# Twelve of sixteen k-tiles of an attention's input projections in sums, instead of ten, in a two-layer kernel on Trainium2

## The chip, the cores and the metric

The kernel runs on one core of one Trainium2 chip. The metric is the device time of one execution in microseconds. Before the change it was 1580.58 us, the median of three runs (1579.58 to 1581.96).

The engines are named as the profile names them: PE is TensorE (matmuls; PEld is its loading of weights), DVE is VectorE, ACT is ScalarE, POOL is GpSimd and SP is SyncE. Here SP only issues DMAs, and POOL issues those that add into their destination, beside a few others.

## What is computed

Two layers work on 256 tokens of 2048 values in float32: a Mamba-2 mixer, and then attention with a forget gate. The change lies in the input projections of the attention. Cut to what matters:

```python
def forgetting_attention_mixer(h, w_in, b_forget, w_out):
    proj = h @ w_in                       # 256 x 2048 times 2048 x (4 * 4096 + 32)
    q, k, v, z = proj[..., :4 * 4096] in four parts of 4096 columns
    f_logit = proj[..., 4 * 4096:]
    cum = cumsum(log_sigmoid(f_logit + b_forget))
    logits = q @ k.T / sqrt(128) + cum[i] - cum[j], causal
    o = softmax(logits) @ v               # 32 heads of 128
    return (o * silu(z)) @ w_out

def reference(x, ...):
    x = x + mamba2_mixer(rmsnorm(x, norm_w[0]), ...)
    x = x + forgetting_attention_mixer(rmsnorm(x, norm_w[1]), ...)
    return rmsnorm(x, final_norm_w)
```

## The kernel before

**Precision.** Every large product is made of three: a float32 operand is split into a high part, rounded to the matmul's type, and a low part that holds the rest; hi x hi, hi x lo and lo x hi are added up in PSUM. For a weight tile `wh` is the high part, written by ACT (line 106), and `wl` the low part, written by DVE (line 112). `wh` has five buffers and `wl` four. A weight tile comes from memory into `raw`, which has seven buffers.

**Groups and blocks.** The attention's projections are done in eight groups of four heads. A group has two blocks: the q/k block gives 512 columns of q and 512 of k, the v/z block the same of v and z. A block is a product of 256 tokens x 2048 with 2048 x 1024. The 2048 are 16 k-tiles of 128. Between the groups stand the output projections of earlier groups (tile `psa`), and the softmax of the group before runs beside the next group's blocks.

**Sums.** Part of a block is done by a scheme with seven products instead of eight. Two k-tiles, two halves of the tokens and two halves of the columns (left and right) form a 2 x 2 by 2 x 2 product of blocks. It is replaced by seven products of sums of blocks. The sums of activations ("forms", `gh`/`gl`) are made once for the layer; the sums of weights are made for every block, in three chains:

- chain a: load term 0 (step `A0`), add term 1 (`A1`), add chain b (`A3`), add term 2 (`A2`);
- chain b: load term 3 (`B0`), add term 1 (`B1`);
- chain c: load term 2 (`C0`).

After every step the sum is split into `wh` and `wl` and multiplied with one form: three products of 512 columns a pair of k-tiles. An added term comes by a DMA from POOL that adds into the sum (line 198); chain b is added on DVE (line 200). A set of two pairs (four k-tiles) is one tile of 128 x 1024; each step runs over the block's sets in turn.

Ten k-tiles (`KS = 10`) are in sums in groups 1 to 7: two sets of two pairs and a third of one pair, whose tiles are 128 x 512. For the third set, term 1 is loaded once into a tile `term`, and DVE adds it into a (line 196) and adds b into it (line 193), so that it need not be loaded twice. The third set's `sum_a` and `sum_b` lie in the sixth buffer of the forms, which five pairs leave free. Group 0 has two sets only (`KS0 = 8`), since the forms of the ninth and tenth k-tile are made late, beside group 0 (`late_form`). The other k-tiles are plain: a "left half" (`"L"`) or "right half" (`"R"`) is two k-tiles x 512 columns, 12 matmuls into two PSUM tiles.

**What sets the order.** A block's order of steps is written out by hand:

```python
    STEPS = (A0, C0, "L", B0, "L", A1, "L", A3, "R", "R", "R", B1, A2)
    SECOND = (A0, C0, "L", B0, "L", "L", A1, "L", A3, "R", "R", "R", B1, A2, "R")
```

`FIRST` is the q/k block of group 0, `SECOND` its v/z block, and `STEPS` all others. `run` goes through the parts and prepares the weights of a part (its load, its add, `wh` and `wl`) three parts ahead (`AHEAD = 3`). A scheduler below it then orders each engine's instructions and places the waits: an instruction may move ahead of others where its inputs allow it. Each engine works through its own queue in order. The softmax's pieces are events on a clock that parts advance (`"long"`).

The results of a block leave PSUM in five pieces: x after A0 and again after A3 and B1, u after A1, v after the last left half, z and u after the last right half (`right`), and y at the end (`last`).

Of the kernel before, what the change touches and what calls it, by code (L numbers as in the profile page):

```python
# [45 lines left out]
KS = 10  # L46
# [23 lines left out]
def hybrid_kernel(ctx: ExitStack, tc: tile.TileContext, a):  # L70
# [101 lines left out]
    def prep_sum(u):  # L172


        name, src, how = u["chain"]
        wide = u.get("wide", 1024)
        if how == "load":
            if u.get("apart"):
                t = fp[0].tile([P, 1024], F32, tag="sum", name=f"sum_{name}")
            elif wide < 1024 and name != "c":  # L180
                t = gp.tile([P, 7, P], F32, tag="gh" if (name == "a") == u["even"] else "gl",
                            name=f"sum_{name}").rearrange("p m s -> p (m s)")
            else:
                t = wp.tile([P, 1024], F32, tag="raw", name=f"sum_{name}", bufs=RAW)
            u["sums"][name] = t[:, :wide]
            nc.sync.dma_start(u["sums"][name], src)
            if wide < 1024 and name == "c":
                u["sums"]["t"] = t = fp[0].tile([P, wide], F32, tag="term", name="term")
                nc.sync.dma_start(t, u["term"])
        elif how == "add" and "term" in u:  # L190
            t = u["sums"]["t"]
            if name == "b":
                nc.vector.tensor_tensor(t, t, u["sums"]["b"], op=ALU.add)
                u["sums"]["b"] = t
            else:
                nc.vector.tensor_tensor(u["sums"][name], u["sums"][name], t, op=ALU.add)
        elif how == "add":
            behind["POOL"] = nc.gpsimd.dma_start(u["sums"][name], src, accum_op=ALU.add).ins  # L198
        else:
            nc.vector.tensor_tensor(u["sums"][name], u["sums"][name], u["sums"][how], op=ALU.add)  # L200
        raw = u["sums"][name]
        wh = wp.tile([P, 1024], F32R, tag="wh", name="wh")[:, :wide]
        wl = wp.tile([P, 1024], F32R, tag="wl", name="wl", bufs=4)[:, :wide]
        act_hi(wh, raw)
        behind["DVE"] = dve_lo(wl, raw, wh).ins
        u["w"][0] = (wh, wl)
        yield
# [161 lines left out]
    def ktile(x, k):  # L369

        q = max(i for i in range(5) if X_AT[i] <= k)
        return x[q][:, k - X_AT[q]]
# [579 lines left out]
    def late_form():  # L952

        f = fp[0].tile([P, T2, 1024], F32, tag="vz", name="form", bufs=2)
        f = f.rearrange("p t c -> p (t c)")[:, :7 * P].rearrange("p (m s) -> p m s", m=7)
        for i in range(2):
            hi, lo = (ktile(lay2["x"], KS0 + i)[:, j].rearrange("p (t s) -> p t s", t=T2)
                      for j in range(2))
            nc.vector.tensor_tensor(blocks(f, True, i), hi, lo, op=ALU.add)
        split_form(f, True, lay2["forms"], 0, f"x{KS0 // 2}")  # L960
# [58 lines left out]
    STEPS = (A0, C0, "L", B0, "L", A1, "L", A3, "R", "R", "R", B1, A2)  # L1019
    SECOND = (A0, C0, "L", B0, "L", "L", A1, "L", A3, "R", "R", "R", B1, A2, "R")  # L1020
    FIRST = (0, "L", "L", 1, "L", A0, C0, B0, "L", "enter", A1, A3, "R", "R", "R", B1, A2, "R")

    def block_units(w_s, w_p, out, scale, done, order):
# [7 lines left out]
        pairs = (2, 2, 1)[:len(w_s)]  # L1031
        n_l = KT - 2 * len(w_p[0])
        steps = [0]
# [20 lines left out]
        def mm_sum(u, form, name, p2):  # L1054
            wh, wl = u["w"][0]
            first = start(name)
            for i, w in enumerate((wh, wh, wl)):
                for p in range(pairs[p2]):
                    y = lay2["forms"][0][2 * p2 + p][i % 2]
                    product(ps[name], y[:, form, :], w[:, p * 512:p * 512 + 512],  # L1060
                            start=first and i == p == 0,
                            stop=i == 2 and (p2, p + 1) == (len(pairs) - 1, pairs[-1]),
                            skip_group_check=True)
# [31 lines left out]
        for step in order[0]:  # L1095
# [6 lines left out]
            if step in n_rest:  # L1102
                n = n_rest[step]
                n_rest[step] += 1
                names = ("v", "y") if step == "L" else ("z", "u")
                u = us[step]
                parts.append({"u": u, "h": [n],
                              "mm": lambda u=u, n=n, names=names: mm_rest(u, n, names)})
                if n + 1 == len(u["w"]) and step == "L":
                    parts[-1]["post"] = left if order[0] is not SECOND else (  # L1110
                        lambda: [left(), later(1, late_form)])
# [24 lines left out]
    def four_heads(hq, first=()):  # L1136
# [139 lines left out]
        def weights(n):  # L1276
            s1, s2 = a["wf_s"][hq, n], a["wf_h"][hq, n]
            half = lambda c, m: a["wf_p"][hq, n, c][:, m * 1024:m * 1024 + 1024]
            rest = [[half(c, m) for m in range((KT - KS) // 2)] for c in range(2)]
            if hq == 0:  # L1280
                return [s1[0], s1[1]], [[a["wf_b"][n, c], *rest[c]] for c in range(2)]
            return [s1[0], s1[1], s2], rest
# [92 lines left out]
def packed(x, norm_w, m_w_in, m_conv_w, m_conv_b, m_dt_bias, m_A_log, m_D,  # L1375
# [21 lines left out]
    def tiles_b(left, right):  # L1397

        w = np.stack([left.reshape(D, G, 512), right.reshape(D, G, 512)], 2)
        s = w[:KS0 * P].reshape(KS0 // 4, 2, 2, P, G, 2, 512).transpose(4, 0, 2, 5, 3, 1, 6)
        h = w[KS0 * P:KS * P].reshape(2, P, G, 2, 512).transpose(2, 0, 3, 1, 4)
        r = w[KS * P:].reshape(KT - KS, P, G, 2, 512).transpose(2, 3, 1, 0, 4)
        b = w[KS0 * P:KS * P, 0].reshape(2, P, 2, 512).transpose(2, 1, 0, 3)
        return (f(s).reshape(G, KS0 // 4, 4, P, 1024), f(h).reshape(G, 4, P, 512),
                f(r).reshape(G, 2, P, (KT - KS) * 512), f(b).reshape(2, P, 1024))

# [18 lines left out]
    def by_k(w):  # L1428
# [13 lines left out]
        "wf_s": np.stack([qk[0], vz[0]], 1), "wf_h": np.stack([qk[1], vz[1]], 1),  # L1442
        "wf_p": np.stack([qk[2], vz[2]], 1), "wf_b": np.stack([qk[3], vz[3]]),
# [19 lines left out]
```

## Time and profile before

| | |
|---|---|
| time, median of 3 | 1580.58 us (1579.58 to 1581.96) |
| the profiled execution | 1580.13 us |
| its span, first to last instruction | 1578.4 us |
| granted TensorE clock | 0.998 |
| busy: PE, DVE, ACT, POOL | 99%, 87%, 69%, 11% |
| read from memory | 360.83 MB |

One execution of the program was recorded by the hardware profiler; its times are in us from the first instruction. The groups of the view by line give, behind the bar, the busy time, the mean ns of one instruction, and the idle time of the engine ahead of them with what ended it. A window gives the busy time of each engine in a stretch. The timeline gives a start, a time and the number of like instructions in a row; the chain of waits gives the same for what ended last. The DMA rows give the size and the median time from issue to landing. The attention's input projections run from about 690 us to 1506 us.

### The profile page before, as it was taken

Reading aid. Unit: us, or ns where it says so; the run is one execution under the profiler, and the core shown is the slowest. Engines: PE = TensorE matmul, PEld = TensorE weight load, DVE = VectorE, ACT = ScalarE, POOL = GpSimd, SP = SyncE. Lnnn points to the kernel's source line nnn. Section 1 sums busy time; section 2 is a strip of 40 time slices with the busy share of each in tenths; the row PEclk is TensorE's granted clock in tenths of the full one; section 3 lists DMA queues with packets and bytes.
Section 4 is the critical chain, followed back from the end, with each engine's and each line's share of the span. In section 5 each row is a group of like instructions: output and inputs, shape, how many; then the busy total and the mean of one; then the engine's idle time right before and its main releaser. Section 6 shows DMA issues by size and latency. Waiting matters only on the chain.

```text
span 1578.4 us, 22860 instructions
## 1 busy us (share of the span) xinstructions
PE 1566.1 (99%) x7768; PEld 1320.7 (84%) x7768; DVE 1377.8 (87%) x2061; ACT 1087.1 (69%) x1710; POOL 178.1 (11%) x225
## 2 busy tenths in 40 slices
PE   9999999999999999999999999999999999999997
PEld 7888888888888888878888888888888888888886
DVE  6998989798989898799888898888888888989886
ACT  7677676767666765766776675776676675777764
POOL 0000111011100110011101110110110111011100
PEclk9999999999999999999999999999999999999999
DMA  9665798769886987579889788788886986899852
GB/s 363 211 204 197 183 275 220 262 177 277 220 271 171 274 227 230 182 170 279 241 250 286 181 239 269 219 230 262 222 262 210 258 271 165 249 276 249 251 175 80
DMA packets 106405, 364.54 MB, mean 231 GB/s; under 512 B 12176, under 2 KB 13072, under 8 KB 106160
## 3 DMA queue, kind: packets, MB, share of 16 engines
q1 hardware_dynamic: 79344, 270.03, 48.5%
q0 software_dynamic: 26800, 92.91, 30.8%
q8 instruction: 61, 1.00, 0.2%
q14 instruction: 56, 0.46, 0.1%
q10 hardware_dynamic: 144, 0.13, 0.0%
HBM read 360.83 MB, written 2.20 MB: 230 GB/s over the span
## 4 chain that ended last, share of the span: by engine, by line
PE 97%; DVE 1%; issue 0%; DMA 0%; ACT 0%; SPq 0%; ACTq 0%; POOLq 0%; POOL 0%
PE psa L132 24%; PE pst L132 17%; PE psx L132 14%; PE psz L132 10%; PE psv L132 9%; PE psu L132 8%; PE psy L132 8%; PE py L715 2%; PE pqk L1182 1%; PE psc L1200 1%; PE ppt L1232 1%; PE po L1258 0%; PE psc L1198 0%; PE pxa L665 0%; PE pyt L778 0%; PE pz L1237 0%
## 5 line engine op out<-in xcount | busy, mean ns | idle before, releaser
L112 DVE TENSOR_TENSOR wl<-raw,wh 128x1024 fp32r<-128x1024 f32 (+2 forms) x343 | 411.8, 1211 | 51.7 <-issue 21.0
L106 ACT ACTIVATE wh<-raw 128x1024 fp32r<-128x1024 f32 (+2 forms) x343 | 356.5, 1052 | 144.0 <-PE psa L132 53.8
L106 ACT ACTIVATE wh<-sum_a 128x1024 fp32r<-128x1024 f32 (+1 forms) x232 | 220.1, 953 | 132.0 <-PE psu L132 36.8
L112 DVE TENSOR_TENSOR wl<-sum_a,wh 128x1024 fp32r<-128x1024 f32 (+1 forms) x232 | 250.2, 1091 | 14.6 <-PE psa L132 5.0
L132 PE MATMUL pst<-x,wh 128*128 128x512 f32 (+1 forms) x800 | 204.3, 396 | 0.9 <-DVE wh L161 0.7
L132 PEld LDWEIGHTS pst<-x,wh 128*128 128x128 f32 (+1 forms) x800 | 145.7, 189 | 30.5 <-ACT x L108 1.4
L132 PE MATMUL psa<-wh,x 128*128 128x512 f32 x512 | 128.7, 391 | 0.0
L112 DVE TENSOR_TENSOR wl<-sum_b,wh 128x1024 fp32r<-128x1024 f32 (+1 forms) x102 | 115.1, 1146 | 5.8 <-ACT wh L106 3.9
L106 ACT ACTIVATE wh<-sum_b 128x1024 fp32r<-128x1024 f32 (+1 forms) x102 | 100.1, 1004 | 26.6 <-PE psa L132 10.5
L132 PEld LDWEIGHTS pst<-x,wl 128*128 128x128 f32 x768 | 106.3, 191 | 9.0 <-DVE wl L112 0.7
L132 PEld LDWEIGHTS psa<-wh,x 128*128 128x128 f32 x512 | 95.5, 188 | 19.7
L132 PE MATMUL pst<-x,wl 128*128 128x256 f32 x768 | 109.3, 283 | 0.0
L198 POOL DMA_DIRECT2D sum_a<-in_wf_s x64 | 55.4, 865 | 407.9 <-DMA raw<-in_wf_p 103.5
L132 PE MATMUL psz<-wh,x 128*128 128x512 f32 x200 | 78.6, 393 | 0.0
L132 PE MATMUL psv<-wh,x 128*128 128x512 f32 x200 | 78.1, 391 | 0.0
L132 PE MATMUL psu<-wh,x 128*128 128x512 f32 x200 | 78.0, 390 | 0.0
L132 PE MATMUL psy<-wh,x 128*128 128x512 f32 x200 | 77.9, 390 | 0.0
L132 PE MATMUL psx<-wh,ghx 128*128 128x512 f32 x234 | 77.7, 399 | 0.0
L106 ACT ACTIVATE wh<-sum_c 128x1024 fp32r<-128x1024 f32 (+1 forms) x58 | 54.5, 954 | 31.8 <-PE psa L132 17.4
L132 PE MATMUL psx<-wh,glx 128*128 128x512 f32 x234 | 75.9, 390 | 0.0
L132 PE MATMUL psx<-wl,ghx 128*128 128x512 f32 x234 | 75.6, 390 | 0.0
L816 DVE TENSOR_TENSOR xs<-psa,xs 128x512 f32<-128x512 f32 (+1 forms) x81 | 51.9, 679 | 22.6 <-PE psa L132 22.2
(365 smaller groups left out, 3390.3 us busy)
## 6 DMA issues: line engine op xcount, KB each, us to landing
raw<-in_wf_p SPq DMA_DIRECT2D x96, 512.0 KB, 5.2
raw<-in_wm_t SPq DMA_DIRECT2D x90, 512.0 KB, 5.1
raw<-in_wm_z SPq DMA_DIRECT2D x64, 512.0 KB, 5.6
sum_a<-in_wf_s POOLq DMA_DIRECT2D x64, 512.0 KB, 8.5
raw<-in_wf_o SPq DMA_DIRECT2D x64, 512.0 KB, 5.8
sum_a<-in_wm_s POOLq DMA_DIRECT2D x36, 512.0 KB, 5.9
sum_a<-in_wf_s SPq DMA_DIRECT2D x32, 512.0 KB, 6.7
sum_c<-in_wf_s SPq DMA_DIRECT2D x32, 512.0 KB, 9.3
```

Of the source, the lines that this page charges most:

```text
L106: nc.scalar.activation(out, in_, AF.Copy)
L112: return nc.vector.tensor_tensor(out, in_, hi.bitcast(F32), op=ALU.subtract)
L132: behind["PE"] = nc.tensor.matmul(*args, **kw).ins
L198: behind["POOL"] = nc.gpsimd.dma_start(u["sums"][name], src, accum_op=ALU.add).ins
L715: nc.tensor.matmul(st["py"][t][:, c], m[:, j, t, :], st["xd"][:, t, c], start=True, stop=True)
L816: nc.vector.tensor_tensor(c, pss[t][:, a:b], c, op=ALU.add)
L1182: nc.tensor.transpose(pt[:, n * P:n * P + P], st["qk"][:, t, c:c + FD], ident)
L1200: nc.tensor.matmul(ps[:, P:P + S], q[:, :P], k[:, P:], start=j == 0, stop=j == 2)
L1232: nc.tensor.transpose(pt[:, c:c + P], uu[:, c:c + P], ident)
```

## The change

Twelve k-tiles are in sums from group 1 on, so the third set is as wide as the others (two pairs, 128 x 1024), and a block of these groups has two left and two right halves instead of three of each.

- The third set's tiles change place. Its `sum_a` and `sum_b` take turns between the place `x3` (which held the activations of k-tiles 10 and 11 in group 0) and the place `sum` in the attention's pool, which before held the first set's `sum_b`. The first set's `sum_b` now takes a `raw` buffer, except in the v/z block of group 0.
- Its term 1 is kept in two tiles of 128 x 512, and both adds go into the chain's own tile: `sum_a += term`, `sum_b += term`, each in two instructions. Before, b was added into `term`.
- `late_forms` makes the forms of two pairs (k-tiles 8 to 11) instead of one.
- The steps are in another order. In `STEPS` B0 follows C0 at once, A3 follows A1 at once, and the halves stand as L, then L R R. In `SECOND` the last right half goes ahead of A2, and `right` is called behind it.
- Every step of a sum advances the softmax's clock by one.
- In memory the weights are packed for it; their number of bytes is the same.

```diff
-KS = 10
+KS = 12
...
         name, src, how = u["chain"]
-        wide = u.get("wide", 1024)
         if how == "load":
-            if u.get("apart"):
-                t = fp[0].tile([P, 1024], F32, tag="sum", name=f"sum_{name}")
-            elif wide < 1024 and name != "c":
-                t = gp.tile([P, 7, P], F32, tag="gh" if (name == "a") == u["even"] else "gl",
-                            name=f"sum_{name}").rearrange("p m s -> p (m s)")
+            if "place" in u:
+                t = (bp if u["place"] == "x3" else fp[0]).tile(
+                    [P, 1024], F32, tag=u["place"], name=f"sum_{name}")
             else:
                 t = wp.tile([P, 1024], F32, tag="raw", name=f"sum_{name}", bufs=RAW)
-            u["sums"][name] = t[:, :wide]
-            nc.sync.dma_start(u["sums"][name], src)
-            if wide < 1024 and name == "c":
-                u["sums"]["t"] = t = fp[0].tile([P, wide], F32, tag="term", name="term")
-                nc.sync.dma_start(t, u["term"])
+            u["sums"][name] = t
+            nc.sync.dma_start(t, src)
+            if "term" in u:
+                u["sums"]["t"] = ts = (fp[0].tile([P, 512], F32, tag="term", name="term"),
+                                       sp.tile([P, 512], F32, tag="zth", name="term"))
+                for i, t in enumerate(ts):
+                    nc.sync.dma_start(t, u["term"][:, i * 512:(i + 1) * 512])
         elif how == "add" and "term" in u:
-            t = u["sums"]["t"]
-            if name == "b":
-                nc.vector.tensor_tensor(t, t, u["sums"]["b"], op=ALU.add)
-                u["sums"]["b"] = t
-            else:
-                nc.vector.tensor_tensor(u["sums"][name], u["sums"][name], t, op=ALU.add)
+            for i, t in enumerate(u["sums"]["t"]):
+                c = u["sums"][name][:, i * 512:(i + 1) * 512]
+                nc.vector.tensor_tensor(c, c, t, op=ALU.add)
...
-    STEPS = (A0, C0, "L", B0, "L", A1, "L", A3, "R", "R", "R", B1, A2)
-    SECOND = (A0, C0, "L", B0, "L", "L", A1, "L", A3, "R", "R", "R", B1, A2, "R")
+    STEPS = (A0, C0, B0, "L", A1, A3, "L", "R", "R", B1, A2)
+    SECOND = (A0, C0, "L", B0, "L", "L", A1, "L", A3, "R", "R", "R", B1, "R", A2)
...
-        pairs = (2, 2, 1)[:len(w_s)]
...
-                for p in range(pairs[p2]):
+                for p in range(2):
...
-            for p2 in range(len(pairs)):
-                u = {"chain": (chain, w_s[p2][term], how), "sums": sums[p2], "w": [None],
-                     "wide": 512 * pairs[p2], "even": order[2],
-                     "apart": chain == "b" and p2 == 0 and order[0] is not FIRST}
-                if pairs[p2] == 1 and (chain == "c" or term == 1):
-                    u["term"] = w_s[p2][1]
-                steps[0] += pairs[p2] == 1
-                parts.append({"u": u, "h": [0], "long": 1 if pairs[p2] == 2 else steps[0] % 2,
+            for p2 in range(len(w_s)):
+                u = {"chain": (chain, w_s[p2][term], how), "sums": sums[p2], "w": [None]}
+                if order[0] is SECOND and chain == "b" and p2 == 0:
+                    u["place"] = "sum"
+                if p2 == 2:
+                    if chain == "c" or term == 1:
+                        u["term"] = w_s[p2][1]
+                    if chain != "c":
+                        u["place"] = "x3" if (chain == "a") == order[2] else "sum"
+                parts.append({"u": u, "h": [0], "long": 1,
```

Where the instructions go is shown at two places. The first is DVE's queue in the v/z block of group 3, from the second set's A3 add on. Before (`sum_a_10155` and `sum_b_10265` are the third set, `raw` the plain halves):

```order
L200 TENSOR_TENSOR sum_a_10143<-sum_a_10143,sum_b_10248 128x1024
L112 TENSOR_TENSOR wl_10354<-raw_10352,wh_10353 128x1024
L1223 RECIPROCAL psum__10329<-psum__10329 128x2
L112 TENSOR_TENSOR wl_10370<-sum_a_10131,wh_10369 128x1024
L200 TENSOR_TENSOR sum_a_10155<-sum_a_10155,sum_b_10265 128x512
L112 TENSOR_TENSOR wl_10381<-sum_a_10143,wh_10380 128x1024
L112 TENSOR_TENSOR wl_10390<-sum_a_10155,wh_10389 128x512
L1050 SCALAR_TENSOR_TENSOR vz3_10201<-psv_10209,rstH2_6855,vz3_10201 128x512
L112 TENSOR_TENSOR wl_10408<-raw_10406,wh_10407 128x1024
```

With the change, the same stretch (`sum_a_10107` and `sum_b_10208` are the third set):

```order
L196 TENSOR_TENSOR sum_a_10095<-sum_a_10095,sum_b_10176 128x1024
L112 TENSOR_TENSOR wl_10294<-sum_a_10083,wh_10293 128x1024
L1215 TENSOR_SCALAR mx_10306<-mx_10306 128x2
L112 TENSOR_TENSOR wl_10315<-sum_a_10095,wh_10314 128x1024
L1222 RECIPROCAL psum__10307<-psum__10307 128x2
L196 TENSOR_TENSOR sum_a_10107<-sum_a_10107,sum_b_10208 128x1024
L192 TENSOR_TENSOR sum_b_10208<-sum_b_10208,term_10147 128x512
L192 TENSOR_TENSOR sum_b_10208<-sum_b_10208,term_10148 128x512
L112 TENSOR_TENSOR wl_10329<-sum_a_10107,wh_10328 128x1024
L112 TENSOR_TENSOR wl_10341<-raw_10339,wh_10340 128x1024
```

The split of a plain half has moved from the middle of the stretch to its end, the third set's add and split are wide, and the two adds of the term into `sum_b` stand ahead of the third set's A3 split.

The second place is SP's queue at the start of the v/z block of group 2. Before (`in_wf_h` is the third set, `raw` a plain half):

```order
L186 DMA sum_a_9078<-in_wf_s 128x1024
L186 DMA sum_a_9102<-in_wf_h 128x512
L186 DMA sum_a_9090<-in_wf_s 128x1024
L186 DMA sum_c_9112<-in_wf_s 128x1024
L186 DMA sum_c_9125<-in_wf_s 128x1024
L186 DMA sum_b_9183<-in_wf_s 128x1024
L186 DMA sum_c_9137<-in_wf_h 128x512
L189 DMA term_9139<-in_wf_h 128x512
L153 DMA raw_9150<-in_wf_p 128x1024
```

With the change (`sum_a_9076`, `sum_c_9114` and `sum_b_9177` are the third set):

```order
L188 DMA term_9116<-in_wf_s 128x512
L183 DMA sum_a_9052<-in_wf_s 128x1024
L183 DMA sum_a_9064<-in_wf_s 128x1024
L183 DMA sum_c_9089<-in_wf_s 128x1024
L183 DMA sum_c_9102<-in_wf_s 128x1024
L183 DMA sum_c_9114<-in_wf_s 128x1024
L183 DMA sum_a_9076<-in_wf_s 128x1024
L183 DMA sum_b_9132<-in_wf_s 128x1024
L183 DMA sum_b_9145<-in_wf_s 128x1024
L183 DMA sum_b_9177<-in_wf_s 128x1024
L153 DMA raw_9189<-in_wf_p 128x1024
```

The third set's `sum_a` has moved from the second place to behind the three c loads, and the first plain half from ahead of the later b loads to behind all of them.

More of the change, by code (lines that the diff above doesn't have):

```diff
@@ L201, in prep_sum @@
         raw = u["sums"][name]
-        wh = wp.tile([P, 1024], F32R, tag="wh", name="wh")[:, :wide]
-        wl = wp.tile([P, 1024], F32R, tag="wl", name="wl", bufs=4)[:, :wide]
+        wh = wp.tile([P, 1024], F32R, tag="wh", name="wh")
+        wl = wp.tile([P, 1024], F32R, tag="wl", name="wl", bufs=4)
         act_hi(wh, raw)
@@ L950, in form_x, with late_forms @@
             split_form(lay2["f"][q], True, lay2["forms"], 0, f"x{q}")
[L952 to L960, printed above, removed]
+    def late_forms():
+        v = fp[0].tile([P, T2, 1024], F32, tag="vz", name="form", bufs=2)
+        for q in range(KS0 // 2, KS // 2):
+            f = v[:, q % 2, :7 * P].rearrange("p (m s) -> p m s", m=7)
+            for i in range(2):
+                hi, lo = (ktile(lay2["x"], 2 * q + i)[:, j].rearrange("p (t s) -> p t s", t=T2)
+                          for j in range(2))
+                nc.vector.tensor_tensor(blocks(f, True, i), hi, lo, op=ALU.add)
+            split_form(f, True, lay2["forms"], 0, f"x{q}")
     def stats2():
@@ L1030, in block_units @@
               for i, c in enumerate("LR")}
-        pairs = (2, 2, 1)[:len(w_s)]
         n_l = KT - 2 * len(w_p[0])
-        steps = [0]
         def start(name):
@@ L1061, in mm_sum @@
                             start=first and i == p == 0,
-                            stop=i == 2 and (p2, p + 1) == (len(pairs) - 1, pairs[-1]),
+                            stop=i == 2 and (p2, p) == (len(w_s) - 1, 1),
                             skip_group_check=True)
@@ L1108, in block_units @@
                               "mm": lambda u=u, n=n, names=names: mm_rest(u, n, names)})
+                if n + 1 == len(u["w"]) and step == "R" and order[0] is SECOND:
+                    parts[-1]["post"] = right
                 if n + 1 == len(u["w"]) and step == "L":
                     parts[-1]["post"] = left if order[0] is not SECOND else (
-                        lambda: [left(), later(1, late_form)])
+                        lambda: [left(), later(1, late_forms)])
                 continue
             chain, term, how, form, name = step
-            for p2 in range(len(pairs)):
-                u = {"chain": (chain, w_s[p2][term], how), "sums": sums[p2], "w": [None],
-                     "wide": 512 * pairs[p2], "even": order[2],
-                     "apart": chain == "b" and p2 == 0 and order[0] is not FIRST}
-                if pairs[p2] == 1 and (chain == "c" or term == 1):
-                    u["term"] = w_s[p2][1]
-                steps[0] += pairs[p2] == 1
-                parts.append({"u": u, "h": [0], "long": 1 if pairs[p2] == 2 else steps[0] % 2,
+            for p2 in range(len(w_s)):
[8 more added lines that the diff above has]
+                parts.append({"u": u, "h": [0], "long": 1,
                               "mm": lambda u=u, form=form, name=name, p2=p2:
@@ L1276, in weights @@
         def weights(n):
-            s1, s2 = a["wf_s"][hq, n], a["wf_h"][hq, n]
-            half = lambda c, m: a["wf_p"][hq, n, c][:, m * 1024:m * 1024 + 1024]
-            rest = [[half(c, m) for m in range((KT - KS) // 2)] for c in range(2)]
+            w_s = a["wf_s"][hq, n]
+            halves = lambda w: [w[:, m * 1024:m * 1024 + 1024] for m in range(2)]
+            rest = [halves(a["wf_p"][hq, n, c]) for c in range(2)]
             if hq == 0:
-                return [s1[0], s1[1]], [[a["wf_b"][n, c], *rest[c]] for c in range(2)]
-            return [s1[0], s1[1], s2], rest
+                return [w_s[0], w_s[1]], [halves(a["wf_b"][n, c]) + rest[c] for c in range(2)]
+            return [w_s[i] for i in range(3)], rest
         return [block_units(*weights(n), out, scale, done,
@@ L1402, in tiles_b @@
         w = np.stack([left.reshape(D, G, 512), right.reshape(D, G, 512)], 2)
[L1403 to L1404 removed]
+        s = w[:KS * P].reshape(KS // 4, 2, 2, P, G, 2, 512).transpose(4, 0, 2, 5, 3, 1, 6)
         r = w[KS * P:].reshape(KT - KS, P, G, 2, 512).transpose(2, 3, 1, 0, 4)
[L1406 to L1408 removed]
+        b = w[KS0 * P:KS * P, 0].reshape(KS - KS0, P, 2, 512).transpose(2, 1, 0, 3)
+        return (f(s).reshape(G, KS // 4, 4, P, 1024), f(r).reshape(G, 2, P, 2048),
+                f(b).reshape(2, P, 2048))
     def tiles_s(w):
@@ L1441, in packed @@
         "wm_o": tiles_o(wo)[4 * SUMMED:], "wm_s": tiles_s(wo)[:SUMMED],
-        "wf_s": np.stack([qk[0], vz[0]], 1), "wf_h": np.stack([qk[1], vz[1]], 1),
-        "wf_p": np.stack([qk[2], vz[2]], 1), "wf_b": np.stack([qk[3], vz[3]]),
+        "wf_s": np.stack([qk[0], vz[0]], 1), "wf_p": np.stack([qk[1], vz[1]], 1),
+        "wf_b": np.stack([qk[2], vz[2]]),
         "wf_f": by_k(wf[:, 4 * E:]), "wf_o": tiles_o(wg),
```

## The prediction

> **What bounds the kernel now.** I read the page's busy shares and chain first, then the waits of PE in the attention, then the windows of one group.
>
> ```profile
> span 1578.4 us, 22860 instructions
> ...
> PE 1566.1 (99%) x7768; PEld 1320.7 (84%) x7768; DVE 1377.8 (87%) x2061; ACT 1087.1 (69%) x1710; POOL 178.1 (11%) x225
> ...
> PE 97%; DVE 1%; issue 0%; DMA 0%; ACT 0%; SPq 0%; ACTq 0%; POOLq 0%; POOL 0%
> ```
>
> The chain that ends last is PE for 97% of the span. The waits of PE between 690 and 1500 us are a heading with no row under it, so in the stretch that the change touches PE never waits. Two of the five windows that run from one group's output projection to the next:
>
> ```profile
> core 0: us, PE busy (x) PEld busy (x) DVE busy (x) ACT busy (x) POOL busy (x), PEclk, DMA share, GB/s
> 863.61:974.50 110.89, 110.89 (x527) 92.80 (x527) 96.91 (x134) 75.65 (x115) 13.57 (x16) 1.00 0.83 237
> 974.50:1085.39 110.89, 110.89 (x527) 92.80 (x527) 96.93 (x134) 75.60 (x115) 13.59 (x16) 1.00 0.83 238
> ```
>
> A group takes 110.89 us, all of it PE at a granted clock of 1.00. VectorE (DVE) is second: 96.9 busy, 14.0 idle. So what PE is spared is gained, as long as VectorE, with more to do, stays ahead.
>
> **What is removed.** The price of a matmul comes from unbroken runs in the chain of waits:
>
> ```profile
> 863.61 10.89 PE psa L132 x48
> ...
> 974.50 10.89 PE psa L132 x48
> ```
>
> 10.89 / 48 = 0.227 us each; the 0.39 us of a single row is its latency. Two k-tiles cost 24 matmuls of 512 columns as plain halves (12 left, 12 right), and 21 in sums (seven products of three). Before, a block of groups 1 to 7 has five pairs in sums and six plain halves, 5 x 21 + 6 x 12 = 177; after, 6 x 21 + 4 x 12 = 174. Three fewer in 14 blocks are 42, and PE's order has 42 rows of that kind fewer. 42 x 0.227 = **9.5 us off PE**. A larger gain is excluded: PE has no idle time there to recover. Group 0 keeps its matmuls; one right half moves ahead of A2.
>
> **What is added on VectorE.** Durations and steps:
>
> ```profile
> L112 DVE TENSOR_TENSOR wl<-sum_a,wh 128x1024 fp32r<-128x1024 f32 x126 | 152.5, 1220 | 6.6 <-PE psa L132 2.1 <-PE psu L132 1.6 <-PE psz L132 1.0
> L112 DVE TENSOR_TENSOR wl<-sum_a,wh 128x512 fp32r<-128x512 f32 x56 | 38.4, 686 | 8.0 <-ACT wh L106 4.8 <-PE psa L132 3.0
> L200 DVE TENSOR_TENSOR sum_a<-sum_a,sum_b 128x1024 f32<-128x1024 f32 x32 | 38.9, 1219 | 0.2
> ...
> 899.27 3.49 DVE L112 TENSOR_TENSOR wl<-raw,wh 128x1024 fp32r<-128x1024 f32 x3
> ...
> 812.68 0.69 DVE L112 TENSOR_TENSOR wl<-sum_c,wh 128x512 fp32r<-128x512 f32 x1
> 813.28 0.68 DVE L112 TENSOR_TENSOR glf<-form,ghf 128x512 fp32r<-128x512 f32 x1
> ```
>
> Three wide instructions in a row take 3.49, so one costs (3.49 - 1.22) / 2 = 1.135 us of the engine's time, and a narrow one 813.28 - 812.68 = 0.60. Per block the third set's seven splits become wide (+7 wide, -7 narrow), two plain halves go (-2 wide), the A3 add widens (+1, -1), and the two adds of the kept term take two narrow instructions each (+2 narrow): +6 wide, -6 narrow, or 6 x 0.535 = 3.2 us a block, 6.4 a group, 45 us in all. A group then needs 96.9 + 6.4 = 103.3 us of VectorE against 110.89 - 6 x 0.227 = 109.5 of PE. On the mean it is covered, the idle time falling from 14.0 to 6.2. Without that cover it would cost the full 45.
>
> **Where the cover is thin.** Steps A1 and A3 now stand side by side, and a plain left half that lay between them comes after. Six splits, three A3 adds and four narrow adds are 9 x 1.135 + 4 x 0.60 = 12.6 us of VectorE against 36 matmuls, 8.2 us: it falls 4.4 us back. Before, A1, L and A3 were 7 wide and 3 narrow for splits and A3 adds and 2 narrow for the term, 11.0 us against 42 matmuls, 9.5: 1.4 back. What it can fall back is the lead, from a split's end to PE's first use of it. For A1's first split in the two blocks of one group:
>
> ```profile
> 887.88 1.22 DVE L112 TENSOR_TENSOR wl<-sum_a,wh 128x1024 fp32r<-128x1024 f32 x1 [0.19 <-PE psz L132]
> ...
> 893.29 0.61 PE L132 MATMUL psu<-wl,ghx 128*128 128x512 f32 x2
> ...
> 931.23 1.23 DVE L112 TENSOR_TENSOR wl<-sum_a,wh 128x1024 fp32r<-128x1024 f32 x1
> ...
> 937.81 0.61 PE L132 MATMUL psu<-wl,ghx 128*128 128x512 f32 x2
> ```
>
> 893.29 - 889.10 = 4.2 and 937.81 - 932.46 = 5.4 us. So 4.4 is just about what is there. Bounds of the stall a block: none if the lead is 5.4 (some narrow adds also float out of the stretch), 1.2 if it is 3.2, that is, a microsecond less than the smaller row, as when VectorE meets one wait like this on the way:
>
> ```profile
> 886.11 0.17 DVE L1223 RECIPROCAL psum__8817<-psum__8817 128x2 f32<-128x2 f32 x1 [1.05 <-ACT dd L1218]
> ```
>
> Over 14 blocks that is 0 to 17 us. I take 0.2 a block, **2.8 us**, the shortfall of the smaller lead. Queued behind a late A3 split are, on VectorE, the plain halves' splits and the adds out of PSUM; PE would wait for the split alone, since the plain halves behind it give the lead back (3 x 12 matmuls, 8.2 us, against 3.4 of splits).
>
> **The moved loads.** A third-set load was issued here, and its product started here:
>
> ```profile
> 897.27 0.33 SPq L186 DMA_DIRECT2D sum_a<-in_wf_h  x1
> ...
> 921.54 0.39 PE L132 MATMUL psx<-wh,ghx 128*128 128x512 f32 x1
> ...
> sum_a<-in_wf_s SPq DMA_DIRECT2D x32, 512.0 KB, 6.7
> ...
> sum_a<-in_wf_h SPq DMA_DIRECT2D x14, 256.0 KB, 8.0
> ...
> DMA to landing us min/median/max: 2.5/7.7/14.7
> ```
>
> 24 us ahead. Now it shares a buffer with the block before: in the v/z block the third `sum_a` takes the place where the q/k block's third `sum_b` stays until B1 is split; on SP it has moved behind three c loads, and the three b loads are queued behind its wait. From that split (about 5 us before PE's use) PE has six parts of 1.36, so the load has some 13 us, less 1.06 for ScalarE, 1.22 for VectorE and a lead of 3: 8 us, against medians of 6.7 and 8.0. Bounds: 0, and, at a landing of 14.7 (the longest of that tensor), 14.7 - 8 - 3 = 3.7 us in 7 blocks, 26. I take 0, by the medians. `raw` keeps seven buffers, but two b sums live there from B0 to B1 instead of one, which leaves three for streaming, while fewer plain halves stream: 0, with the same cover.
>
> ScalarE gains 70 wide splits and loses 98 narrow, 70 x 1.056 - 98 x 0.628 = 12.4 us, 1.8 a group on 75.7; hidden. Rows:
>
> ```profile
> L106 ACT ACTIVATE wh<-sum_a 128x1024 fp32r<-128x1024 f32 x126 | 132.1, 1056 | 87.2 <-PE psu L132 35.9 <-PE psa L132 19.6 <-DMA sum_a<-in_wf_s 10.5
> L106 ACT ACTIVATE wh<-sum_a 128x512 fp32r<-128x512 f32 x56 | 35.1, 628 | 20.2 <-DVE sum_a L200 8.3 <-PE psz L132 7.7 <-DMA sum_a<-in_wf_h 2.6
> ...
> q1 hardware_dynamic: 79344, 270.03, 48.5%
> q0 software_dynamic: 26800, 92.91, 30.8%
> ```
>
> Bytes are equal, but 14 adding loads on POOL's queue double to 512 KB: 3.7 MB move from 0.18% of the engines a MB to 0.33%, 0.6% more on a share of 83%. No term; at worst it lengthens landings, which the load's bound holds. POOL's order stays, but that in the v/z blocks of groups 1 and 7 A2's first load goes between B1's two, whose second then waits for A3's first split: 0, at most 1 each, since B1's product is 8 us of halves away. One-offs lie in group 0: the second late form is seven VectorE instructions, some 3 us once, and the first load into the place `x3` waits for PE's last use of k-tiles 10 and 11, with 48 matmuls (10.9 us) still ahead of its own product against the 8 us of a landing: 0 for both, at most 3 and 5.
>
> **Sum.** The profiled execution took 1580.1 us, 0.5 under the median of 1580.6. 1580.1 - 9.5 + 2.8 = 1573.4; I say **1573.5**, and its own range is 1570 to 1578.
>
> **Rivals.**
> *Loads late* (0.20): where landing takes 12 us instead of 8, each v/z block loses about 1.0 beyond its lead, 7 us more: 1580.4. For: VectorE's releases hold SP's queue already, and the third load loses half its head start. Against: PE never waited for a DMA here. Even with before at 0.96 us a v/z block.
> *The lead runs out* (0.15): A1 and A3 meet a lead of 3.2 and one more half-microsecond of order waits: 1.7 us in 14 blocks, 23.8, so 1594.4, **slower**. For: groups 6 and 7 have no output projection between them to refill the lead, and the reciprocal's 1.05 recurs. Against: the smaller lead seen is 4.2. It decides from 9.5 / 14 = 0.68 us a block.
> *VectorE without overlap* (0.03): if its 134 instructions each cost their whole duration, 0.085 more, a group needs at most 96.9 + 11.4 + 6.4 = 114.7 and VectorE sets the pace, 5.2 x 7 over PE's time: 1607. Against it stand the three in 3.49 us.
> The Trainium skill, VectorE: DVE Perf Modes, under The DRAIN you can't avoid, says that the next operation does not start until the pipe is empty, which would be this case; the 3.49 us do not bear it out for back-to-back instructions.
>
> **How the numbers follow.** About 0.2% (3.2 us) is what a measurement tells from no change. The forecast has 0.62, of which 0.60 lies below 1577.4 and 0.02 within the bound. Late loads give 0.06 faster, 0.11 same, 0.03 slower; the lead 0.02 same, 0.13 slower; no overlap 0.03 slower. Together faster 0.66, same 0.15, slower 0.19. The range starts at 1569.5, the 9.5 us whole and a microsecond of scatter as in the three times shown, and goes to 1588, into the slower case up to 1.2 us a block, leaving out about a tenth above.
>
> **What would show it.** Windows from one output projection to the next of 109.5 to 110.2 us, VectorE near 103 in them, and no PE wait, or waits of tenths for `wl` at A3's third part: the forecast. PE waiting for `wh` or `wl` of the third `sum_a` behind a DMA, in v/z blocks alone: the loads. Waits for `wl` of over 0.7 us in both blocks: the lead. It is wrong in its first step if the run of 48 is not 10.89 or the count of matmuls is not 42 lower.

## The result and the profile after

The changed kernel takes 1597.2 us (median of five, 1596.6 to 1598.6) against 1580.7 us for the kernel before: slower, ratio 1.0104, 95% interval 1.0092 to 1.0115. Forecast were 1573.5 us, from 1569.5 to 1588. The profiled execution took 1597.1 us.

The page of the changed kernel, to be held against the one before (PE x7768, DVE 1377.8, PE 97% of the chain):

```profile
span 1595.3 us, 22674 instructions
...
PE 1566.3 (98%) x7726; PEld 1311.3 (82%) x7726; DVE 1420.4 (89%) x2068; ACT 1095.3 (69%) x1683; POOL 178.1 (11%) x225
...
PE 5%; issue 1%; DVE 1%; DMA 1%; ACT 0%; POOL 0%; ACTq 0%; POOLq 0%; DVEq 0%
```

The 42 matmuls are gone, and VectorE has 42.6 us more to do (45 forecast). The chain of waits now covers less than a tenth of the span, so it carries little. The windows from one output projection to the next (of four, the first and the last; columns as in the prediction's windows) show the loss (before: 110.89, all of it PE):

```profile
856.06:967.73 111.67, 110.20 (x521) 91.57 (x520) 104.05 (x136) 78.29 (x115) 13.58 (x16) 1.00 0.84 238
...
1192.89:1305.97 113.08, 110.69 (x522) 91.50 (x520) 102.97 (x134) 76.83 (x112) 13.61 (x16) 1.00 0.83 238
```

A group should take 109.5 us and takes 111.7 to 113.1, though VectorE's 103 is what was forecast. The waits of PE between 690 and 1530 us, an empty list before, name the place (columns: in total, times, longest):

```profile
PE psx L132 <- ACT wh L106: 7.1, 5, 1.6
PE po L1254 <- ACT ph L106: 2.8, 2, 1.5
PE po L1257 <- ACT p L1244: 2.6, 4, 0.8
```

There are five waits of the first kind, one in each of groups 2 to 6, in the v/z block, ahead of the third part of A3. The rest lies at the attention's own products, above all in groups 1 and 7. The whole loss is larger than the list, all rows of which sum to 15.4 us, since short delays of a matmul's start do not show as waits there. From the output projection that starts at 650 us to the last one the changed kernel takes 861.3 us (650.15 to 1511.49), the kernel before 845.1 (650.02 to 1495.09). With the 9.5 that PE is spared, it loses some 26 us: 1580.1 - 9.5 + 26 = 1597.

The timeline of the changed kernel around the first of the five (in order of time, from B0's loads and L's to PE's wait; line numbers of the changed kernel lie up to five lower than those of before):

```profile
915.26 4.34 SPq L183 DMA_DIRECT2D sum_b<-in_wf_s  x3
925.54 2.60 SPq L153 DMA_DIRECT2D raw<-in_wf_p  x3
...
928.07 1.05 ACT L106 ACTIVATE wh<-sum_b 128x1024 fp32r<-128x1024 f32 x1
932.20 1.06 ACT L106 ACTIVATE wh<-raw 128x1024 fp32r<-128x1024 f32 x1 [3.08 <-DMA raw<-in_wf_p]
933.16 0.36 ACT L106 ACTIVATE ph<-ppt 128x256 fp32r<-128x256 f32 x1
...
933.56 0.42 DVE L112 TENSOR_TENSOR pl<-ppt,ph 128x256 fp32r<-128x256 f32 x1 [2.37 <-ACT ph L106]
...
936.31 1.22 DVE L112 TENSOR_TENSOR wl<-sum_a,wh 128x1024 fp32r<-128x1024 f32 x1
...
941.01 0.62 PE L132 MATMUL psu<-wl,ghx 128*128 128x512 f32 x2
...
945.98 1.21 DVE L196 TENSOR_TENSOR sum_a<-sum_a,sum_b 128x1024 f32<-128x1024 f32 x1
...
947.38 1.04 ACT L106 ACTIVATE wh<-sum_a 128x1024 fp32r<-128x1024 f32 x1
...
948.45 1.23 DVE L112 TENSOR_TENSOR wl<-sum_a,wh 128x1024 fp32r<-128x1024 f32 x1
...
948.47 0.73 PE L132 MATMUL psx<-wh,ghx 128*128 128x512 f32 x2 [1.41 <-ACT wh L106]
```

The plain left half L is asked for only at 925.54, when the split of c, which ends at 925.52, has freed its place in `raw`. ScalarE reaches L's split at 929.12, stands for 3.08 us until the half lands, and `ph`, a copy of the attention's that has nothing to do with L, stands behind it. VectorE, which should be gathering a lead, stands for 2.37 behind `ph`. Then A1 and A3 come side by side, use up what lead there is, and PE stops. PE's wait names ScalarE's `wh`, which ScalarE could write only after VectorE's A3 add (945.98 to 947.19); read further up, the first thing to be late is L, whose DMA was issued 23 us before PE stopped. So the waits to look at are ScalarE's for DMA, over the same four groups; first before, then changed:

```profile
ACT wh L106 <- DMA raw<-in_wf_p: 6.2, 4, 1.9
ACT wh L106 <- DMA sum_b<-in_wf_s: 0.7, 1, 0.7
```

```profile
ACT wh L106 <- DMA raw<-in_wf_p: 13.1, 4, 3.7
ACT wh L106 <- DMA sum_a<-in_wf_s: 5.3, 4, 1.6
ACT wh L106 <- DMA raw<-in_wf_o: 1.1, 1, 1.1
```

That is 6.9 us against 19.5. It led to the theory **too few streaming buffers**: two b sums in `raw` leave three places, and L behind all of B0 finds none free in time. Against it stood **adjacency** (A1 and A3 side by side drain VectorE's lead), **VectorE's work** (45 us more, whatever the order) and **due times** (the attention's steps meet a shorter block).

### The profile page after: what moved, and what is told of

Same layout as the page of the kernel before. It is cut to its first block, busy times and chain, and to the rows that moved or that the text cites. A ratio compares the mean times of both kernels' runs of the same rounds, so it can differ in the third digit from the quotient of the medians.

```text
span 1595.3 us, 22674 instructions
## 1 busy us (share of the span) xinstructions
PE 1566.3 (98%) x7726; PEld 1311.3 (82%) x7726; DVE 1420.4 (89%) x2068; ACT 1095.3 (69%) x1683; POOL 178.1 (11%) x225
## 5 line engine op out<-in xcount | busy, mean ns | idle before, releaser
L112 DVE TENSOR_TENSOR wl<-raw,wh 128x1024 fp32r<-128x1024 f32 (+2 forms) x315 | 377.6, 1208 | 47.1 <-issue 20.8
L106 ACT ACTIVATE wh<-sum_a 128x1024 fp32r<-128x1024 f32 x232 | 242.8, 1058 | 147.5 <-DVE sum_a L196 37.2
L112 DVE TENSOR_TENSOR wl<-sum_a,wh 128x1024 fp32r<-128x1024 f32 x232 | 280.7, 1218 | 16.6 <-ACT wh L106 9.8
L106 ACT ACTIVATE wh<-sum_b 128x1024 fp32r<-128x1024 f32 x116 | 120.8, 1056 | 44.3 <-PE psa L132 11.5
L112 DVE TENSOR_TENSOR wl<-sum_b,wh 128x1024 fp32r<-128x1024 f32 x116 | 139.5, 1217 | 7.9 <-ACT wh L106 6.1
L106 ACT ACTIVATE wh<-sum_c 128x1024 fp32r<-128x1024 f32 x58 | 59.6, 1052 | 23.5 <-PE psa L132 14.4
L132 PE MATMUL psa<-wh,ghf 128*128 128x512 f32 (+1 forms) x260 | 71.0, 392 | 0.0
L132 PE MATMUL psa<-wl,x 128*128 128x512 f32 x256 | 69.2, 390 | 1.0 <-DVE wl L112 1.0
L132 PE MATMUL psa<-wh,glf 128*128 128x512 f32 (+1 forms) x260 | 69.6, 386 | 0.0
L132 PE MATMUL psa<-wl,ghf 128*128 128x512 f32 (+1 forms) x260 | 69.6, 386 | 0.0
```

The lines of the kernel that those rows point to most:

```text
L106: nc.scalar.activation(out, in_, AF.Copy)
L112: return nc.vector.tensor_tensor(out, in_, hi.bitcast(F32), op=ALU.subtract)
L132: behind["PE"] = nc.tensor.matmul(*args, **kw).ins
```

## The experiments

Each kernel ran beside the kernel before on the same chip; the ratios are to that.

**The order put back, in parts (e1, e2, e3), and the work taken off (e4).**

```diff
-    STEPS = (A0, C0, B0, "L", A1, A3, "L", "R", "R", B1, A2)
+    STEPS = (A0, C0, B0, "L", A1, "L", A3, "R", "R", B1, A2)       # e1
+    STEPS = (A0, C0, "L", B0, A1, A3, "L", "R", "R", B1, A2)       # e2
+    STEPS = (A0, C0, "L", B0, A1, "L", A3, "R", "R", B1, A2)       # e3
```

> The changed kernel with the second left half put between A1 and A3, as a half stood there before; all else stays, the first half behind B0 too. If the splits of A1 and A3 side by side cost the time (adjacency), nearly all of the 26 us of waits goes: 1571 to 1577 us. If it is the plain half's late load (the half stands behind all of B0, with three buffers to stream through), the load is as late as in the changed kernel and the time stays at 1593 to 1600. If it is VectorE's 45 us of added work as such, the order matters little: 1590 to 1600.

> The changed kernel with the first left half put ahead of B0, as before; A1 and A3 stay side by side. Late load: its buffer is asked for three parts earlier and the wait for it goes: 1572 to 1580 us. Adjacency: 1593 to 1600, as in the changed kernel. VectorE's work as such: 1590 to 1600.

> The changed kernel with both edits: the first left half ahead of B0 and the second between A1 and A3, which is the order of before with one half fewer. Late load or adjacency: 1571 to 1575 us, the 9.5 us whole. VectorE's work as such: 1588 or more.

Measured: e1 1615.1 us (ratio 1.0225, 1.0208 to 1.0242), e2 1607.2 (1.0172, 1.0157 to 1.0187), e3 1634.9 (1.0342, 1.0326 to 1.0357). Nothing here was expected: each step towards the old order costs 10 to 38 us more than the changed kernel. e2's trace says why for the late load. L is early now, and PE's five waits at A3 are gone, but ScalarE stands somewhere else, with `ph` behind it again, and PE now waits at the attention's products (the timeline of e2, ScalarE's waits for DMA over four groups in e2, and the same in e3):

```profile
934.23 2.01 ACT L106 ACTIVATE wh<-sum_b 128x1024 fp32r<-128x1024 f32 x2 [5.95 <-DMA sum_b<-in_wf_s]
```

```profile
ACT wh L106 <- DMA sum_b<-in_wf_s: 25.7, 9, 5.9
ACT wh L106 <- DMA sum_a<-in_wf_s: 8.1, 5, 2.4
```

```profile
ACT wh L106 <- DMA sum_b<-in_wf_s: 51.1, 11, 6.2
```

With three places a load is late in each of these orders, and the order chooses which: L, or the b load that SP issues last, now behind L. My expectation for e2 overlooked that; it was the wrong test of a theory that could still be right. In e1 L is as late as in the changed kernel (a wait of 3.04 us), and PE's longest waits, 2.7 to 3.7 us in groups 2 to 6, are at the attention's products; that part was not followed.

```diff
+        elif how == "add" and "term" in u:
+            pass
         elif how == "add" and "term" in u:
```

> The changed kernel with the narrow adds of the kept term left out (its loads stay), so the third set's sums lack that term: four VectorE instructions of 0.6 us less in each of 14 blocks, 34 us. VectorE's work as such: 45 us added become 11, and the waits of 26 us shrink to a few: 1572 to 1578 us. Late load: 1592 to 1598, since no load moves. Adjacency: the 4.4 us that VectorE falls back become 2.0, and most of the waits go: 1574 to 1584.

Measured: 1594.6 us (1.0090, 1.0075 to 1.0105). VectorE falls from 1420.4 to 1389.2 us, and 2.5 of 31 us come back. So VectorE's work as such is not what the changed kernel waits for in the main. Adjacency had expected a gain as well. Where L is late, VectorE with less to add only stands longer behind `ph`, 3.10 us in group 2 instead of 2.37, and A3's third split comes no earlier. But the total hides two parts: in the profiled executions groups 2 to 7 are 9.7 us shorter than in the changed kernel (861.90 to 1507.64 against 856.06 to 1511.49) and what lies ahead of them is 5.8 us longer, with waits of PE of up to 2.6 us there that were not followed. So the work has some share in the loss as long as buffers are short.

**A place for the first b sum (e5), and its control (e6).** There was no room for an eighth buffer, so room was made.

```diff
+                if order[0] is STEPS and chain == "b" and p2 == 0:
+                    u["place"] = "sum1"                                  # e5 alone
-                u["sums"]["t"] = ts = (fp[0].tile([P, 512], F32, tag="term", name="term"),
+                u["sums"]["t"] = ts = (sp.tile([P, 512], F32, tag="zth", name="term"),   # e5, e6
-                st["form"] = fp[0].tile([P, 4, P], F32, tag="form", name="form", bufs=2)
+                st["form"] = fp[0].tile([P, 4, P], F32, tag="form", name="form", bufs=1)
```

> The changed kernel with a place of its own for the first set's b sum in groups 1 to 7, so that raw has four buffers for streaming again; to make room, the attention's form has one buffer instead of two and both halves of the kept term go to the narrow side tiles. The order of the steps is the changed kernel's. Too few streaming buffers (loads issued late, ScalarE and VectorE standing behind them): the waits of PE in the v/z blocks go, 1571 to 1580 us. A misfit of the attention's due times with the shorter block: the waits stay where they are, 1592 to 1600. VectorE's work as such: 1590 or more.

> The control for the run with a place of its own: the changed kernel with the form in one buffer and the term's halves in the side tiles, and nothing put into the room. Every theory: within 3 us of the changed kernel, 1594 to 1601 us; more only if the form or the side tiles are waited for, which would then also sit in the run with a place of its own.

Measured: e5 1578.9 us (0.9985, 0.9976 to 0.9995), e6 1591.7 (1.0071, 1.0054 to 1.0087). The place alone is worth 12.8 us. One of e5's windows, and ScalarE's waits for DMA over its four groups:

```profile
852.38:961.92 109.54, 109.54 (x522) 91.69 (x520) 104.01 (x136) 78.79 (x115) 13.60 (x16) 1.00 0.87 247
```

```profile
ACT wh L106 <- DMA sum_a<-in_wf_s: 1.0, 1, 1.0
```

The group takes 109.54 us, all of it PE, with the order of the changed kernel and with VectorE's added work whole, 104 us here. That is the group as forecast. This rules out VectorE's work and adjacency as causes that act alone. L's load is issued 8.1 us earlier in the group than in the changed kernel (913.74 - 852.38 = 61.4 us from the group's start, against 925.54 - 856.06 = 69.5; the next three groups show 8.1 to 8.4), and nobody waits for it. It lands 5.6 us after its issue here and 6.6 there, so most of the difference is the issue (SP, ScalarE, VectorE, PE):

```profile
913.74 0.33 SPq L153 DMA_DIRECT2D raw<-in_wf_p  x1
...
925.58 1.06 ACT L106 ACTIVATE wh<-raw 128x1024 fp32r<-128x1024 f32 x1
...
930.07 1.23 DVE L112 TENSOR_TENSOR wl<-sum_a,wh 128x1024 fp32r<-128x1024 f32 x1
...
942.38 1.23 DVE L112 TENSOR_TENSOR wl<-sum_a,wh 128x1024 fp32r<-128x1024 f32 x1
...
937.34 0.62 PE L132 MATMUL psu<-wl,ghx 128*128 128x512 f32 x2
...
944.14 0.62 PE L132 MATMUL psx<-wl,ghx 128*128 128x512 f32 x2
```

The lead of VectorE is 937.34 - 931.30 = 6.0 us at A1's first part and 944.14 - 943.61 = 0.5 at A3's third. So adjacency drains 5.5 us, and 0.5 is left. In the changed kernel 2.5 us had been taken out of the same lead by L's being late (941.01 - 937.53 = 3.5 left at A1's first part), and it did not reach: 3.5 - 5.5 is 2.0 us short, and the window is 111.67 - 109.54 = 2.1 us longer.

The control is itself 5.5 us faster than the changed kernel, which was not expected. **Which of its two edits (e13)?**

```diff
-                u["sums"]["t"] = ts = (fp[0].tile([P, 512], F32, tag="term", name="term"),
+                u["sums"]["t"] = ts = (sp.tile([P, 512], F32, tag="zth", name="term"),
```

> The changed kernel with only one of the two edits of the room-alone control: both halves of the kept term in the side tiles, the form in two buffers as before. The control gained 5 us on the changed kernel. If SP's queue standing at the single tile of the term (up to 11 us at a time) was what cost them: 1590 to 1593 us here too. If it was the form: 1595 to 1599.

Measured: 1594.2 us (1.0080, 1.0065 to 1.0095), between the two and with an interval that reaches into e6's. SP's queue does stand less at the term's load (for the add of the block before, L188 behind L192; first the changed kernel from 690 to 1530 us, then e6):

```profile
SPq L188 <- DVE sum_b L192: 109.9, 11, 11.1
```

```profile
SPq L188 <- DVE sum_b L192: 60.2, 12, 10.9
```

e13's row is e6's, 60.2. So this wait can account for the 2.9 us that e13 gains, and not for all of the 5.5; whether it does, and what the rest is, stays open.

**One part of the change in the kernel before (e7, e8).**

```diff
-            if u.get("apart"):
+            if False:                                                    # e7
-    STEPS = (A0, C0, "L", B0, "L", A1, "L", A3, "R", "R", "R", B1, A2)
+    STEPS = (A0, C0, "L", B0, "L", A1, A3, "L", "R", "R", "R", B1, A2)   # e8
```

> The kernel before with one edit: the first set's b sum goes to raw like the second's, which leaves three buffers for streaming; steps, tiles and work are those of before. Too few streaming buffers: ScalarE waits for raw and sums in the v/z blocks and PE behind it, 10 us or more above before, 1590 to 1605. A misfit of due times, adjacency or VectorE's work: no change, 1579 to 1583.

> The kernel before with A3 moved right behind A1 and the last left half behind both; five pairs, tiles and work as before. Adjacency: VectorE falls back by 6 wide, 3 narrow splits and adds and more against 8.2 us of PE, and the waits come in both blocks: 1585 to 1595 us. Too few streaming buffers or VectorE's work: 1579 to 1584. A misfit of due times: the halves' two units move past A3, so some waits at the attention's products, 1582 to 1590.

Measured: e7 1586.4 us (1.0032, 1.0020 to 1.0043), e8 1581.7 (1.0003, 0.9994 to 1.0013). In the kernel before, adjacency alone costs nothing. Three streaming buffers alone cost 5 us, half of what I had expected, and not where. They lie in the stretches of groups 0 and 1 (3.3 us, with a wait of PE of 1.72) and of groups 6 and 7 (2.1); in between e7's groups run at 110.89 us with no PE wait, although ScalarE waits for DMA longer than in the changed kernel (a window of e7, and ScalarE's waits for DMA over four groups):

```profile
854.88:965.77 110.89, 110.89 (x527) 92.81 (x526) 95.22 (x133) 73.46 (x115) 13.57 (x16) 1.00 0.82 233
```

```profile
ACT wh L106 <- DMA sum_b<-in_wf_s: 11.4, 4, 3.2
ACT wh L106 <- DMA sum_a<-in_wf_s: 8.9, 4, 2.7
ACT wh L106 <- DMA raw<-in_wf_p: 5.8, 5, 1.7
ACT wh L106 <- DMA sum_a<-in_wf_h: 1.3, 3, 0.5
```

27.4 us over four groups are swallowed there; VectorE has 15 idle us a group, and a half lies between A1 and A3. In these groups neither a late load (e7) nor a thin lead (e5, e8) stops PE alone; in the changed kernel they meet.

**The term by POOL's queue (e9), and the order once more, with four streaming buffers (e12).** Both are e5 with one more edit.

```diff
-                    if chain == "c" or term == 1:                        # e9, with the term's
-                        u["term"] = w_s[p2][1]                           # tiles as changed
-    STEPS = (A0, C0, B0, "L", A1, A3, "L", "R", "R", B1, A2)
+    STEPS = (A0, C0, B0, "L", A1, "L", A3, "R", "R", B1, A2)             # e12
```

> The run with a place of its own, and the third set's term added by POOL's queue like the other sets' (two adding loads of 512 KB more a block, one load less, and 56 narrow VectorE adds less, 34 us). If VectorE's added work is what is left in groups 1 and 7 (about 5 us over the 9.5 gained): 1573 to 1576 us. If it is the attention's due times there: 1577 to 1580. If the added bytes make loads late again: 1581 or more, with waits of ScalarE for DMA.

> The run with a place of its own, with the second left half between A1 and A3. In the changed kernel this edit cost 18 us. Too few streaming buffers: with four of them the order matters little, 1576 to 1584 us. If the order itself is what hurts (the attention's due times against the steps): 1588 to 1598 again. Adjacency: faster than the run with a place of its own, 1571 to 1576.

Measured: e9 1596.8 us (1.0105, 1.0085 to 1.0124), e12 1586.4 (1.0042, 1.0027 to 1.0057). One of e9's groups, and ScalarE's waits for DMA over four:

```profile
972.88:1083.85 110.97, 110.19 (x521) 91.74 (x520) 97.58 (x126) 76.16 (x112) 17.03 (x20) 1.00 0.89 245
```

```profile
ACT wh L106 <- DMA sum_b<-in_wf_s: 33.8, 8, 6.1
ACT wh L106 <- DMA sum_a<-in_wf_s: 10.4, 6, 2.9
```

VectorE is back near its old 97 us, and the kernel is as slow as the changed one, because sums arrive late again (44 us against e5's 1.0), as the third of its expectations had it. The longest of these waits, 5.4 to 6.1 us, are for the third set's B1: its adding load goes out only when the A3 add has read b, and in the group shown it lands 11.7 us later (POOL, ScalarE):

```profile
1061.28 0.88 POOL L194 DMA_DIRECT2D sum_b<-in_wf_s  x1 [0.34 <-DVE sum_a L196]
```

```profile
1073.11 1.06 ACT L106 ACTIVATE wh<-sum_b 128x1024 fp32r<-128x1024 f32 x1 [5.66 <-DMA sum_b<-in_wf_s]
```

Whether the added bytes make that landing longer is not told apart by e9 (its DMA share is 0.89, e5's 0.87).

e12 lies 2 us above what too few buffers had expected: with four buffers the edit that cost 18 us in the changed kernel costs 7.6. Much of the harm of e1 was the buffers', and some is the order's own. e12 still has 6.4 us of ScalarE's waits for DMA; why that order keeps them was not followed.

**Groups 1 and 7 (e10, e11, e14, e15).** What is left of PE's waits in e5 lies there, 3.3 us at products of the attention that wait for ScalarE's copy of `p` (e10's expectation below says 3.9). In these groups the heads come six steps apart.

```diff
-            last = max(1 + gap, 6)
+            last = 6 if gap == 6 else max(1 + gap, 6)
-                             (last, turn), (last + 1, keep), (last + 2, values), (last + 3, close)):
+                             (last, turn), (last + 1, keep), (last + 2 + (gap == 6), values),
+                             (last + 3 + (gap == 6), close)):
```

e10 is e5 with this, e11 is e9 with it, e14 the changed kernel and e15 the kernel before with it alone.

> The run with a place of its own, and in groups 1 and 7 (heads six steps apart) each head's transposes one step earlier, so that two steps instead of one lie between the copies of the weights and the product that waits for them; all else of the attention stays. Due times as the rest: the waits of PE for ScalarE's copy of p in groups 1 and 7 (3.9 us) go, 1573 to 1576 us. VectorE's work as the rest: 1577 to 1580. If the transposes now wait for the scaled weights instead: no gain or worse, 1578 to 1583.

> A place of its own, the term by POOL's queue and the products later in groups 1 and 7. If each of the two takes away something of its own: 1571 to 1574 us, the 9.5 us whole. If only one of them acts, the same as that one within 1.5 us.

> The changed kernel with nothing but the later products of groups 1 and 7 (the transposes one step earlier); three buffers for streaming as in it. If the waits of groups 1 and 7 have their own cause: some 5 us less than the changed kernel, 1590 to 1594. If late loads make most of those 9 us too: 1594 to 1598.

> The kernel before with the same edit of the products' times in groups 1 and 7, and nothing else. PE has no wait there to lose: 1579 to 1582 us, no change, so that what the edit gives on the changed kernel is not a gain of its own. Were it faster by 5 us, the last 5 us of the best version would not belong to the sixth pair.

Measured: **e10 1573.9 us (0.9957, 0.9943 to 0.9972)**, faster than both kernels; e11 1593.8 (1.0092, 1.0072 to 1.0112), slow with e9's adding loads and so neither of its two cases; e14 1591.0 (1.0065, 1.0050 to 1.0080); e15 1582.3 (1.0009, 0.9999 to 1.0018). The edit is worth 4.9 us on e5 and 6.2 on the changed kernel and nothing on the kernel before: the due times of these two groups are a cause of their own. That the shorter block makes them late is how I read it: by the counter that the due times go by (a sum's part counts one, a half two; before, the third set's parts one and none in turn) a block counts 29 after and 30 before. No run tells that apart from VectorE's fuller queue. The only wait of PE that e10's trace shows from 690 to 1530 us:

```profile
PE ppt L1234 <- ACT dd L1227: 0.7, 1, 0.7
```

## Why the prediction was wrong, by its steps

**What is removed: right.** 42 matmuls fewer, a group of 109.53 us where PE is not stopped (109.5 forecast), and 1573.9 us in e10. Without any stall the sum is 1580.1 - 9.5 = 1570.6; of the 3.3 us above that e10's trace shows 0.7 as a wait, and the rest was not followed.

**What is added on VectorE: right, and harmless as a sum.** 103 us a group as forecast, hidden in e5 and e10. Taking 31 us of it away from the changed kernel (e4) gave back 2.5 in all, though 9.7 in groups 2 to 7: with buffers short, it has a share.

**The step that failed** is the sentence on `raw`: that two b sums there "leaves three for streaming", priced "0, with the same cover". It measured 12.8 us (e6 to e5). The cover named was that fewer halves stream. But the three c sums pass through the same places ahead of L, as they did before, and L now stands behind all of B0. With three places left its place comes free 69.5 us into the group, when the split of c is done, and with a fourth (e5) at 61.4. I had priced the one load whose place was new (the third `sum_a`) and bounded it by 26 us, and never followed the places of `raw` through a block to ask when each comes free. That one, the third `sum_a`, was rightly put at 0: in e5 all loads of `sum_a` are waited for 1.0 us in four groups. The evidence given against late loads, that PE never waited for a DMA, could not speak: PE waits for splits. ScalarE's waits for DMA, 6.9 us over four groups before, would have.

**Where the cover is thin: right in kind, small in size.** A fall of 4.4 us was forecast and 5.5 measured (e5), against leads of 6.0. Alone it costs nothing (e5's groups, e8). My charge of 0.2 a block was, if anything, too high: four of e5's windows are 109.53 to 109.83 us. What it lacked was that the lead is also what a late load is paid from. The two terms were added as if each had the lead to itself.

**Not on the list:** the attention's due times. I kept them as they were, and in groups 1 and 7 they cost some 5 us (e14, e10). Of the 5.5 us of the control up to 2.9 may be SP's queue standing at the single tile of the term, which the prediction did not price either; this is not shown, and the rest is open. The three, 12.8 + 5.5 + 4.9, are the 23.2 us between the changed kernel and e10; they add up by construction, since each is one step of the way (changed kernel, e6, e5, e10), and the kernel before differs by up to 0.9 us between the chips on which they ran.

**The rivals.** The lead running out gave nearly the number, 1594.4, by luck in part: it has half the mechanism, with the wrong thing draining the lead. No reciprocal is waited for, and the waits stand in v/z blocks alone in groups 2 to 6, not in both. Late loads had the mechanism and its sign, waits for `wh` of the third `sum_a` in v/z blocks alone, with the wrong load and 7 us instead of the 13. VectorE without overlap is out: its group of 114.7 us is not seen, e5's takes 109.54. The Trainium skill, VectorE: DVE Perf Modes, The DRAIN you can't avoid, which the prediction holds against the 3.49 us, goes on to say that an instruction that is not held starts earlier; with that, the page and the trace agree.

## What to carry to other kernels

When a tile moves into a shared rotating pool, follow each place of the pool through one period and note when the next load can be issued; the number of loads says less than the time at which the last place comes free. Where PE waits for nothing, read the waits of the engine that feeds it for DMA, and spend one lead once: a late load and a dense stretch of work draw on the same one. Here the edits that undid the order told little while buffers were still short (e1 to e3): give the resource first, then try the orders.

## What the hardware showed beside

In e1 and e3 long stalls of PE cost more than their length. In e1 the timeline of PE and the window behind a wait of 3.70 us:

```profile
963.54 0.49 PE L1257 MATMUL po<-p,vz 128*128 128x128 f32 x2 [3.70 <-ACT p L1244]
963.78 0.71 PE L132 MATMUL psx<-wh,ghx 128*128 128x512 f32 x2
...
965.80 1.05 PE L132 MATMUL psy<-wh,ghx 128*128 128x512 f32 x2
966.65 1.05 PE L132 MATMUL psy<-wh,glx 128*128 128x512 f32 x2
...
968.21 0.62 PE L132 MATMUL psy<-wh,ghx 128*128 128x512 f32 x2
```

```profile
964.00:968.30 4.30, 4.30 (x14) 3.35 (x13) 3.50 (x5) 3.10 (x5) 0.00 (x0) 0.60 1.02 417
```

Two matmuls take 0.85 us from start to start (965.80 to 966.65) instead of 2 x 0.227, with a granted clock of 0.60 in the window. The twelve from 963.78 to 968.21 take 4.4 us instead of 2.7: 1.7 us more. e1 has five such places and e3 eight, so their times overstate the waits as such. The Trainium skill, TensorE: Matmul & The Clock Gate, Part 1, has the clock halved after an idle window of about 3.4 us; the 3.70 us agree. But e13 shows it after a single wait of 1.59 us as well, with 0.43 us from start to start and a granted clock of 0.53 (timeline of PE, and a window):

```profile
1283.01 0.73 PE L132 MATMUL psx<-wh,ghx 128*128 128x512 f32 x2 [1.59 <-ACT wh L106]
...
1285.22 0.63 PE L132 MATMUL psv<-wh,x 128*128 128x512 f32 x1
1285.65 0.63 PE L132 MATMUL psy<-wh,x 128*128 128x512 f32 x1
```

```profile
1284.80:1288.00 3.20, 3.20 (x9) 2.50 (x8) 3.20 (x4) 2.90 (x4) 1.31 (x2) 0.53 1.02 200
```

The five waits at A3 in the changed kernel, 0.96 to 1.60 us long, were not followed by it. So an idle window of that length is not needed here; what decides it was not followed.
